# A decoder trunk on one core: the residual's transposes, the next stage's first splits and the last store put in a fixed order

## The chip, the cores and the metric

The kernel runs on one core of one Trainium2 chip. The metric is the device time of one execution in microseconds (us). The core has five instruction queues that run side by side and meet at semaphores: TensorE (PE in the profile), VectorE (DVE), ScalarE (ACT), GpSimd (POOL) and SyncE (SP, which issues most DMA transfers). Each queue runs its own instructions in the order in which the program lists them.

## What is computed

The input is a residual stream of 256 tokens by 2048 columns in float32. Four sub-layers follow one another: a state-space mixer, a SwiGLU feed-forward, differential attention, and a second SwiGLU feed-forward. Each is wrapped the same way: an RMS norm ahead of it, an RMS norm behind it, and an addition to the residual.

```
for sub_layer in (ssd_mixer, swiglu_0, diff_attention, swiglu_1):
    x = x + rmsnorm(sub_layer(rmsnorm(x, w_pre)), w_post)

swiglu(h)         = (silu(h @ w_gate) * (h @ w_up)) @ w_down
diff_attention(u) = heads of (softmax(q1 k1) - lam * softmax(q2 k2)) @ v, normed, @ w_out
```

## The kernel before

**Tiling.** The 256 tokens are two blocks of 128, called t=0 and t=1. A weight matrix arrives as raw tiles of 128 partitions by 4x512 columns. Each is split for the matmul into a rounded part and a remainder: a CAST on ACT writes `hi` (L137), a subtraction on DVE writes `lo` (L138). The numbers behind the names (`hi405`, `lo405`) count these splits. A product over 128 rows of the weights is then three matmuls of 512 columns (L191): rounded activations with `hi`, rounded activations with `lo`, and the activations' remainder with `hi`. The texts call one such matmul a row. A raw tile of four such k-steps gives 12 rows for a token block.

**Helpers.** `mv` (L181) takes a list of weight tiles. For each half tile it issues the rows of t=0 at once and puts those of t=1 on a list, which is let out a few half tiles later (`flush`, with `lag`). After each half tile it calls `tick`, which runs whatever was put off with `later(k, fn)`, k half tiles earlier. `ws` is a second form of matrix product, which the attention uses for its queries and keys. The order of instructions on each queue is worked out when the program is built, from the order of the code, from what each instruction depends on and from a model of durations; `tc.issue_after(ins)` holds an instruction behind another one on the same engine.

**The turn to the next sub-layer.** The last product of a sub-layer (`out_proj`) is gathered in `m`, four pieces n of 512 columns. When the last piece of a token block leaves PSUM, `norm_chain` (L672) runs: DVE makes the mean square `ms_post`, POOL takes its power (`rs_post`, L97), DVE updates the residual `x` in four pieces (L682), PE transposes each piece with four 128x128 transposes into `ptx` (L688), and for each 128 columns ACT writes the rounded half of `xT` (L693) and DVE the remainder (L694). `xT0` to `xT3` are four tiles, and rounded half and remainder of 512 columns lie in the same tile. In the program, the ACT piece j+1 of an `xT` tile waits on a semaphore for the DVE piece j of that same tile. `stats` takes the sum of squares of the new residual, four ACT passes with a scrap output (`junk<-x`, L337), a small DVE reduction (`ssx`, L702), `ms_pre` and POOL's `rs_pre`; the next sub-layer needs it only where its first products leave PSUM. The turn happens three times: mixer to feed-forward, feed-forward to attention, attention to feed-forward. They are called turns A, B and C.

**The attention.** There are four groups of heads. In each, `ws` gives queries and keys (`qk`: an ACT copy L1034, a DVE addition L1035 and, for keys, a DVE multiplication L1038). Scores are small matmuls (L1055) into `sc`. Softmax, transposes of the weights (`pp`) and products with `v` (`po`) follow, put off by fixed numbers of half tiles, while PE works on the next product's rows.

**The end.** The last sub-layer runs the same chain with `final` set: no transposes, and each piece of `x` is stored. Piece n=0 is updated by ACT and POOL (L679, L680), the others by DVE (L682).

## Time and profile before

| | us |
|---|---|
| median of 3 runs | 2509.27 (2509.09 to 2509.4) |
| the profiled execution's own time | 2509.47 |
| its span, first to last instruction | 2507.6 |
| outside the span | 1.87 |
| PE busy | 2489.6 (99%) |
| DVE busy | 1936.8 (77%) |
| ACT busy | 1403.2 (56%) |
| POOL busy | 263.8 (11%) |

In the views of the profile a row of the groups gives line, engine, operation, tiles written and read with the buffer numbers left out, count, busy time, mean duration of one in ns, and the idle time of its engine just before with what ended it. A row of the timeline gives the start in us, the duration, the instruction and its count where neighbours are merged, and in brackets the idle time before it and what released it. Matmuls are pipelined, so the duration of one is longer than the distance from one start to the next, and that distance is what a matmul costs.

### The profile page before, as it was taken

The numbers are of one execution on the slowest core, as the hardware profiler recorded it, in microseconds if no ns is written. First come the engines' busy times: TensorE is split into PE (matmuls) and PEld (weight loads), VectorE is DVE, ScalarE is ACT, GpSimd is POOL, SyncE is SP. The second block draws the span as 40 slices with busy tenths as digits, with TensorE's granted clock in tenths as the row PEclk, the third lists the DMA queues.
The fourth block names the chain that finished last, engine by engine and source line by source line (L and its number), as shares of the span: only waits on it lengthen the run. The fifth ranks groups of instructions, "written<-read, shape, count | busy, mean of one in ns | idle before, by whom it ended". The sixth has DMA issues, their size and how long they took to land.

```text
span 2507.6 us, 31493 instructions
## 1 busy us (share of the span) xinstructions
PE 2489.6 (99%) x11818; PEld 2062.5 (82%) x11818; DVE 1936.8 (77%) x2394; ACT 1403.2 (56%) x1895; POOL 263.8 (11%) x242
## 2 busy tenths in 40 slices
PE   9999999999999999999999999999999999999998
PEld 8888888888888888888888888888888888888886
DVE  6877547777688899978987766556688899879985
ACT  5767546665565455545554654455655465546553
POOL 0131000121110010001001100001100100020002
PEclk9999999999999999999999999999999999999999
DMA  7555555555786786868676544544776967686774
GB/s 287 195 171 199 185 191 195 175 179 192 255 275 202 253 256 215 256 209 265 217 247 237 185 171 144 199 167 143 255 234 207 289 223 232 217 265 225 224 247 151
DMA packets 143385, 541.43 MB, mean 216 GB/s; under 512 B 14400, under 2 KB 31104, under 8 KB 116224
## 3 DMA queue, kind: packets, MB, share of 16 engines
q1 hardware_dynamic: 125872, 503.96, 57.7%
q0 software_dynamic: 16992, 35.13, 7.1%
q8 instruction: 93, 1.52, 0.2%
q14 instruction: 60, 0.49, 0.1%
q10 hardware_dynamic: 368, 0.32, 0.1%
HBM read 520.41 MB, written 18.94 MB: 215 GB/s over the span
## 4 chain that ended last, share of the span: by engine, by line
PE 93%; DVE 2%; issue 1%; ACT 1%; DMA 1%; POOL 0%; SPq 0%; DVEq 0%; ACTq 0%; POOLq 0%
PE acc L265 38%; PE acc L191 33%; PE cp L265 9%; PE acc L239 5%; PE acc L241 2%; PE acc L216 2%; DVE lo L138 1%; PE pt_f L326 1%; ACT hi L137 1%; DMA raw<-in_w_g_dram 1%; PE py L607 1%; PE ptx L688 0%; PE po L1102 0%; PE pc L509 0%; PE px L594 0%
## 5 line engine op out<-in xcount | busy, mean ns | idle before, releaser
L138 DVE TENSOR_TENSOR lo<-raw,hi 128x2048 fp32r<-128x2048 f32 (+2 forms) x401 | 728.8, 1821 | 307.8 <-ACT hi L137 300.9
L137 ACT CAST hi<-raw 128x2048 fp32r<-128x2048 f32 (+2 forms) x401 | 604.6, 1511 | 432.9 <-PE acc L191 122.7
L191 PE MATMUL acc<-hi,xT 128*128 128x512 f32 x1792 | 570.3, 394 | 0.0
L265 PE MATMUL acc<-hi,xT 128*128 128x512 f32 x1608 | 518.7, 390 | 0.1
L191 PEld LDWEIGHTS acc<-hi,xT 128*128 128x128 f32 x1792 | 336.0, 188 | 71.4 <-issue 2.2
L265 PEld LDWEIGHTS acc<-hi,xT 128*128 128x128 f32 x1608 | 301.8, 188 | 63.0 <-DVE sx L748 0.5
L191 PE MATMUL acc<-lo,xT 128*128 128x512 f32 x896 | 351.9, 393 | 1.4 <-DVE lo L138 1.4
L265 PE MATMUL acc<-lo,xT 128*128 128x512 f32 x804 | 313.0, 389 | 0.0
L138 DVE TENSOR_TENSOR lo<-rawm,hi 128x2048 fp32r<-128x2048 f32 (+1 forms) x87 | 181.8, 2089 | 35.0 <-ACT hi L137 33.7
L137 ACT CAST hi<-rawm 128x2048 fp32r<-128x2048 f32 (+1 forms) x87 | 152.7, 1755 | 95.6 <-PE acc L265 54.6
L191 PEld LDWEIGHTS acc<-lo,xT 128*128 128x128 f32 x896 | 168.4, 188 | 37.3 <-DVE lo L138 4.9
L239 PE MATMUL acc<-xT,hi 128*128 128x512 f32 x512 | 181.2, 399 | 0.0
L265 PEld LDWEIGHTS acc<-lo,xT 128*128 128x128 f32 x804 | 150.9, 188 | 31.2
L265 PE MATMUL acc<-hi,ah_f 128*128 128x512 f32 x450 | 176.1, 391 | 0.0
L265 PE MATMUL acc<-hi,al_f 128*128 128x512 f32 x450 | 175.2, 389 | 0.0
L265 PE MATMUL acc<-lo,ah_f 128*128 128x512 f32 x450 | 175.1, 389 | 0.0
L265 PE MATMUL cp<-sh,ff 128*128 128x512 f32 x516 | 172.8, 389 | 0.0
L241 PE MATMUL acc<-xT,lo 128*128 128x256 f32 x512 | 142.9, 280 | 0.0
L142 DVE SCALAR_TENSOR_TENSOR lo<-raw,cols,hi 128x512 fp32r<-128x512 f32 x128 | 93.5, 774 | 56.9 <-ACT hi L141 56.5
L141 ACT ACTIVATE hi<-raw,cols 128x512 fp32r<-128x512 f32 x128 | 84.7, 716 | 64.1 <-PE acc L191 42.2
L239 PEld LDWEIGHTS acc<-xT,hi 128*128 128x128 f32 x512 | 96.1, 188 | 22.7
L265 PEld LDWEIGHTS cp<-sh,ff 128*128 128x128 f32 x516 | 96.9, 188 | 20.1
(305 smaller groups left out, 4081.5 us busy)
## 6 DMA issues: line engine op xcount, KB each, us to landing
raw<-in_w_zxbc_dram SPq DMA_DIRECT2D x77, 1024.0 KB, 4.8
raw<-in_w_d_dram SPq DMA_DIRECT2D x98, 512.0 KB, 5.8
raw<-in_w_g_dram SPq DMA_DIRECT2D x96, 512.0 KB, 6.5
raw<-in_w_u_dram SPq DMA_DIRECT2D x96, 512.0 KB, 5.9
raw<-in_w_qkv_dram SPq DMA_DIRECT2D x48, 1024.0 KB, 4.8
raw<-in_w_so_dram SPq DMA_DIRECT2D x32, 1024.0 KB, 4.8
rawm<-in_w_g_dram SPq DMA_DIRECT2D x64, 512.0 KB, 5.9
rawm<-in_w_u_dram SPq DMA_DIRECT2D x64, 512.0 KB, 6.1
```

The costliest lines, as they stand in the source:

```text
L137: nc.scalar.copy(hi, raw)
L138: nc.vector.tensor_tensor(lo, raw, hi.bitcast(F32), op=ALU.subtract)
L141: nc.scalar.activation(hi[:, j], raw[:, j], AF.Copy, scale=scale[j])
L142: nc.vector.scalar_tensor_tensor(lo[:, j], raw[:, j], scale[j], hi[:, j].bitcast(F32), op0=ALU.mult, op1=ALU.subtract)
L191: nc.tensor.matmul(acc[t], a, b[:, j], start=(i == 0 and j == 0 and q == 0), stop=(i == last and j == 1 and q == 2))
L216: nc.tensor.matmul(acc[job, t], a, b[:, j], start=(i == 0 and j == 0 and q == 0), stop=(i == last and j == 1 and q == 2))
L239: nc.tensor.matmul(acc[ct], hi[:, j, cs], x.rearrange("p a s -> p (a s)"), start=(i == 0 and j == 0), stop=False)
L241: nc.tensor.matmul(acc[ct][:, :S], lo[:, j, cs], x[:, 0], start=False, stop=(i == last and j == 1))
L265: nc.tensor.matmul(acc[k], a, b, start=first and q == 0, stop=last and q == 2)
L326: nc.tensor.transpose(pt[:, j], src[:, j * P:(j + 1) * P], ident)
L607: nc.tensor.matmul(py[e * 64:(e + 1) * 64, a], xd[c][:, 2 * a + e], mts[c][:, 2 * a + e], start=True, stop=True)
```

## The change

Line numbers of the changed kernel differ from those of before: the transposes are L738, the `xT` pieces L744 (ACT) and L746 (DVE), the residual's update L715, the splits L151 and L153, rows L204, scores L1152.

- **Turns, token block 0.** The 16 transposes of t=0 stand behind 12 rows and then six more rows of t=1's last product (eight transposes at each place), through `last_row` and through smaller lags (`lag_last`).
- **Turns, token block 1.** The residual's update is put off by three half tiles, and the transposes stand behind rows of t=0's first product of the next sub-layer. `lag_first` shortens the lags of that product.
- **Pieces of `xT`.** The list `chain` holds each ACT piece behind the piece before it, in the order n=0 j=0..3, n=1 j=0..3 and so on, and each DVE piece likewise. The `lo` of the next product's second tile is held behind the first two tiles' DVE pieces; t=1's last evacuation and its update are held behind the next `lo` splits (`behind`).
- **Statistics.** The four sums of squares are held behind the last ACT piece of their token block; the reduction is held behind the last residual update noted.
- **Attention.** The split of the next product's first tile is held behind the last `qk` copy and multiplication (`held`). Transposes and products of the softmax weights come together, at 9 and 10 half tiles; `lam` is worked out later.
- **End.** The last k-step of t=1 in piece n=3 is done in two halves of 256 columns with accumulators of their own, added to `m` one after the other (`halfway`). All updates are on DVE. The last piece is stored in two halves, and odd pieces are stored from ACT's queue.
- The last activation piece of the feed-forward (`act_piece` in `u_evac`) is put off by three half tiles.

```diff
+def lag_last(i):
+    return 2 if i == 7 else LAG
+def lag_first(i):
+    return (2, 3, 3, 4, 5, 6, 7, LAG)[i]
...
     def norm_chain(t, ss4, last_mw, step, final, t512):
...
+        def update():
+            rn = rstd_of(ss4[:, 3:4], D, f"post{step}_{t}", ss4[:, 0:1])
...
+                    with behind(2 if t and not n and not final else None):
+                            turned[1] = nc.vector.scalar_tensor_tensor(xt[:, cs], mw[:, cs], rn, xt[:, cs], op0=ALU.mult, op1=ALU.add)
+                    if final:
+                        (nc.scalar if n % 2 and not cs.start else nc.sync).dma_start(
...
+        if t and not final:
+            later(3, update)
+        else:
+            update()
+        chain = [None, None]
+        def after(k):
+            return tc.issue_after(chain[k]) if chain[k] else nullcontext()
+        def spread(*ns):
+            for n in ns:
+                with tc.issue_after(last_row[0]):
+                    for j in range(4):
+                        tr = nc.tensor.transpose(...)
+                for j in range(4):
+                    with after(0):
+                        chain[0] = nc.scalar.activation(xT_hi[n][:, j, sl], pj, AF.Copy, scale=sc).ins
+                    with after(1):
+                        chain[1] = nc.vector.scalar_tensor_tensor(xT_lo[n][:, j, sl], ...).ins
+        def spread_first():
+            spread(0, 1)
+            held[seq[0] + 1] = None, chain[1]
+            turned[0] = seq[0]
+            pending.popleft()()
+            spread(2, 3)
         def stats():
+            with after(0):
+                for n in range(4):
+                    row_sumsq(st[:, n:n + 1], xres[(t, n)], t512("junk"))
+            with tc.issue_after(turned[1].ins):
+                nc.vector.tensor_reduce(s1_, st, axis=AX.X, op=ALU.add)
...
-            later(5, stats)
+            if t == 0:
+                later(1, spread_first)
+            else:
+                later(4, lambda: spread(0, 1))
+                later(5, lambda: spread(2, 3))
+            later(6, stats)
...
+            if which:
+                mu = nc.vector.tensor_tensor(dst, dst, rstd_bc, op=ALU.mult)
+                if ct == 3:
+                    held[seq[0]] = cp.ins, mu.ins
...
-        later(6, lambda: turn(0, (0, 1)))
-        later(8, lambda: (turn(1, (0,)), weigh(0)))
-        later(10, lambda: turn(1, (1,)))
-        later(11, lambda: weigh(1))
+        later(9, lambda: (turn(0, (0, 1)), turn(1, (0,)), turn(1, (1,))))
+        later(10, lambda: (weigh(0), weigh(1)))
```

What this does to the queues is shown at three places.

**ACT in turn C, before.** These are the `xT` pieces of t=0 from their first on; `ptx` is the transposed residual, and the number in `xT0` to `xT3` is the tile.

```order
L693 ACTIVATE xT0_99<-ptx_14613,cols_91 128x128
L693 ACTIVATE xT1_100<-ptx_14627,cols_91 128x128
L693 ACTIVATE xT0_99<-ptx_14613,cols_91 128x128
L693 ACTIVATE xT2_101<-ptx_14641,cols_91 128x128
L693 ACTIVATE xT0_99<-ptx_14613,cols_91 128x128
L693 ACTIVATE xT3_102<-ptx_14655,cols_91 128x128
L693 ACTIVATE xT1_100<-ptx_14627,cols_91 128x128
L693 ACTIVATE xT2_101<-ptx_14641,cols_91 128x128
L693 ACTIVATE xT0_99<-ptx_14613,cols_91 128x128
L693 ACTIVATE xT3_102<-ptx_14655,cols_91 128x128
L693 ACTIVATE xT1_100<-ptx_14627,cols_91 128x128
L693 ACTIVATE xT2_101<-ptx_14641,cols_91 128x128
```

**ACT in turn C, now.** The same pieces, with `hi411` a CAST of the next product, `m_14349` the copy of t=1's last accumulator and `junk<-m` its sum of squares.

```order
L744 ACTIVATE xT0_99<-ptx_14634,cols_91 128x128 x4
L744 ACTIVATE xT1_100<-ptx_14647,cols_91 128x128 x4
L744 ACTIVATE xT2_101<-ptx_14666,cols_91 128x128
L867 COPY m_14349<-acc_14560 128x512
L744 ACTIVATE xT2_101<-ptx_14666,cols_91 128x128
L368 ACTIVATE junk_14730,ss_m_14351<-m_14349 128x512
L151 CAST hi411_14809<-raw_14807 128x2048
L744 ACTIVATE xT2_101<-ptx_14666,cols_91 128x128 x2
L744 ACTIVATE xT3_102<-ptx_14679,cols_91 128x128 x4
L368 ACTIVATE junk_14753,ss_x_14752<-x_11149 128x512
```

What moved: before, neighbouring pieces belong to different `xT` tiles; now the four pieces of one tile stand next to each other, x4 in a row, and the first sum of squares of the residual (`junk<-x`) stands behind the last of the 16 pieces.

**DVE in turn C, before.** The rows run from the last piece of t=0 but one to t=1's residual update; `ms_post2_1` is t=1's mean square, `x_11153` and `x_11155` are t=1's residual.

```order
L694 SCALAR_TENSOR_TENSOR xT2_101<-ptx_14641,cols_91,xT2_101 128x128
L138 TENSOR_TENSOR lo409_14708<-raw_14705,hi409_14707 128x2048
L694 SCALAR_TENSOR_TENSOR xT3_102<-ptx_14655,cols_91,xT3_102 128x128
L138 TENSOR_TENSOR lo410_14818<-raw_14815,hi410_14817 128x2048
L719 TENSOR_TENSOR mw_14738<-m_14349,wpost_14490 128x512
L138 TENSOR_TENSOR lo411_14849<-raw_14846,hi411_14848 128x2048
L94 TENSOR_SCALAR ms_post2_1_14740<-ss_m_14351 128x1
L682 SCALAR_TENSOR_TENSOR x_11153<-m_14349,rs_post2_1_14742,x_11153 128x512 x2
L682 SCALAR_TENSOR_TENSOR x_11155<-m_14349,rs_post2_1_14742,x_11155 128x512
```

**DVE in turn C, now.** The same stretch, from the first piece of t=0's third tile to t=1's mean square, behind which its residual update now follows.

```order
L746 SCALAR_TENSOR_TENSOR xT2_101<-ptx_14666,cols_91,xT2_101 128x128
L153 TENSOR_TENSOR lo409_14714<-raw_14711,hi409_14713 128x2048
L746 SCALAR_TENSOR_TENSOR xT2_101<-ptx_14666,cols_91,xT2_101 128x128
L786 TENSOR_TENSOR mw_14732<-m_14349,wpost_14490 128x512
L153 TENSOR_TENSOR lo410_14743<-raw_14740,hi410_14742 128x2048
L746 SCALAR_TENSOR_TENSOR xT2_101<-ptx_14666,cols_91,xT2_101 128x128
L153 TENSOR_TENSOR lo411_14810<-raw_14807,hi411_14809 128x2048
L746 SCALAR_TENSOR_TENSOR xT2_101<-ptx_14666,cols_91,xT2_101 128x128
L746 SCALAR_TENSOR_TENSOR xT3_102<-ptx_14679,cols_91,xT3_102 128x128 x4
L764 TENSOR_REDUCE ssx_14761<-ss_x_14752 128x1
L102 TENSOR_SCALAR ms_pre2_0_14763<-ssx_14761 128x1
L102 TENSOR_SCALAR ms_post2_1_14767<-ss_m_14351 128x1
```

What moved: the three `lo` splits now stand between t=0's pieces of `xT2`, and the reduction `ssx` of t=0's sums of squares, which used to follow t=1's update, stands ahead of t=1's `ms_post` and so of its update.

**PE at the first attention group, before.** `hi355` and `lo355` are the last rows of the keys' product, `hi356` and `lo356` the next product's first tile, `sc0` and `sc1` the scores.

```order
L239 MATMUL acc_11917<-xT3_102,hi355_12034 128x512
L241 MATMUL acc_11917<-xT3_102,lo355_12035 128x256
L191 MATMUL acc_12090<-hi356_12086,xT0_99 128x512
L191 MATMUL acc_12090<-lo356_12087,xT0_99 128x512
L191 MATMUL acc_12090<-hi356_12086,xT0_99 128x512 x2
L191 MATMUL acc_12090<-lo356_12087,xT0_99 128x512
L191 MATMUL acc_12090<-hi356_12086,xT0_99 128x512 x2
L191 MATMUL acc_12090<-lo356_12087,xT0_99 128x512
L191 MATMUL acc_12090<-hi356_12086,xT0_99 128x512 x2
L191 MATMUL acc_12090<-lo356_12087,xT0_99 128x512
L191 MATMUL acc_12090<-hi356_12086,xT0_99 128x512
L1055 MATMUL sc0_12103<-qk_12058,qk_11892 128x256
```

**PE at the first attention group, now.** The names are the same, and `qk_11892`, `qk_12058` and so on are queries and keys.

```order
L270 MATMUL acc_11917<-xT3_102,hi355_12034 128x512
L272 MATMUL acc_11917<-xT3_102,lo355_12035 128x256
L1152 MATMUL sc0_12103<-qk_12058,qk_11892 128x256
L1152 MATMUL sc1_12104<-qk_12058,qk_11892 128x256
L1152 MATMUL sc0_12103<-qk_12058,qk_11892 128x256
L1152 MATMUL sc1_12104<-qk_12058,qk_11892 128x256
L1152 MATMUL sc0_12119<-qk_12073,qk_11905 128x256
L1152 MATMUL sc1_12120<-qk_12073,qk_11905 128x256
L204 MATMUL acc_12090<-hi356_12086,xT0_99 128x512
L1152 MATMUL sc0_12109<-qk_12058,qk_11892 128x128
L1152 MATMUL sc1_12110<-qk_12058,qk_11892 128x128
L1152 MATMUL sc0_12109<-qk_12058,qk_11892 128x128
```

What moved: the first scores come right behind the keys' last row, ahead of the 12 rows of `hi356` and `lo356` that used to stand between them.

More of the change, by code (lines that the diff above doesn't have):

```diff
@@ L136, in prep @@
         if scale is None:
[L137 to L138 removed]
+            ca, cd = held.pop(i, (None, None))
+            with tc.issue_after(ca) if ca else nullcontext():
+                nc.scalar.copy(hi, raw)
+            with tc.issue_after(cd) if cd else nullcontext():
+                los[i] = nc.vector.tensor_tensor(lo, raw, hi.bitcast(F32), op=ALU.subtract)
         else:
@@ L178, in flush, with mv, row @@
             pending.popleft()()
-    def mv(blocks, stat, evac, lag, scale=None, loaded=()):
+    def mv(blocks, stat, evac, lag, scale=None, loaded=(), cut=False):
         acc = {}
         last = 2 * len(blocks) - 1
+        def row(*a, **k):
+            after = last_turn[0]
+            last_turn[0] = None
+            with tc.issue_after(after) if after else nullcontext():
+                return nc.tensor.matmul(*a, **k)
         def run(i, t, hi, lo):
@@ L187, in run @@
                 acc[t] = accp.tile([P, 512], F32, tag="acc", name="acc")
-            for j in range(2):
-                xh, xl = stat(i, j, t)
-                for q, (a, b) in enumerate(((xh, hi), (xh, lo), (xl, hi))):
-                    nc.tensor.matmul(acc[t], a, b[:, j], start=(i == 0 and j == 0 and q == 0),
-                                     stop=(i == last and j == 1 and q == 2))
-            if i == last:
+            end = cut and i == last and t == 1
+            if end:
+                evac(t, acc[t])
+            for cs in (slice(0, 256), slice(256, 512)) if end else (slice(0, 512),):
+                if end:
+                    acc[t] = accp.tile([P, 512], F32, tag="acc", name="acc")
+                for j in range(2):
+                    xh, xl = stat(i, j, t)
+                    for q, (a, b) in enumerate(((xh, hi), (xh, lo), (xl, hi))):
+                        r = row(acc[t][:, cs], a, b[:, j, cs],
+                                         start=((i == 0 or end) and j == 0 and q == 0),
+                                         stop=(i == last - (cut and t == 1 and not end) and j == 1 and q == 2))
+                if end:
+                    evac(t, acc[t], cs)
+            last_row[0] = r.ins
+            if i == last and not end:
                 evac(t, acc[t])
@@ L772, in out_proj, with halfway, evac @@
                     pw(n)
-            def evac(t, ps, n=n):
+            def halfway(t, ps, cs):
+                mt = m[(t, 3)]
+                nc.vector.tensor_tensor(mt[:, cs], mt[:, cs], ps[:, cs], op=ALU.add)
+                if cs.start == 0:
+                    last_mw.append(t512("mw"))
+                    sa = small.tile([P, 1], F32, tag="ss1", name="ssh", bufs=3)
+                else:
+                    sa = ss4[t][:, 3:4]
+                row_sumsq(sa, mt[:, cs], t512("junk")[:, cs])
+                if cs.start == 0:
+                    nc.vector.scalar_tensor_tensor(ss4[t][:, 0:1], sa, 1.0 / D, ss4[t][:, 0:1], op0=ALU.mult, op1=ALU.add)
+                nc.vector.tensor_tensor(last_mw[0][:, cs], mt[:, cs], pw(3)[:, cs], op=ALU.mult)
+                if cs.start:
+                    norm_chain(t, ss4[t], last_mw[0], step, final, t512)
+            last_mw = []
+            def evac(t, ps, cs=None, n=n):
+                if cs is not None:
+                    return halfway(t, ps, cs)
+                if final and n == 3 and t == 1:
+                    nc.vector.tensor_tensor(m[(t, n)], m[(t, n)], ps, op=ALU.add)
+                    return
                 if first:
@@ L779, in evac @@
                 else:
-                    nc.vector.tensor_tensor(m[(t, n)], m[(t, n)], ps, op=ALU.add)
+                    with behind(1 if t and n == 3 and last and not final else None):
+                        nc.vector.tensor_tensor(m[(t, n)], m[(t, n)], ps, op=ALU.add)
                 if not last:
@@ L904, in u_evac @@
             nc.vector.scalar_tensor_tensor(g, ps, rs(t), g, op0=ALU.mult, op1=ALU.mult)
-            acts[(t, 10)] = act_piece(g, f"f{step}_10_{t}")
+            later(3, lambda: acts.update({(t, 10): act_piece(g, f"f{step}_10_{t}")}))
         def kp_stat(kp, j, t):
```

83 lines of the change are left out of this document (40 added, 43 removed).

## The prediction

> **What bounds the kernel now.** The page's first part comes first, then PE's own waits, then the timelines around the places that the change touches. PE is the bound:
>
> ```profile
> PE 2489.6 (99%) x11818; PEld 2062.5 (82%) x11818; DVE 1936.8 (77%) x2394; ACT 1403.2 (56%) x1895; POOL 263.8 (11%) x242
> ```
>
> So time can only go by removing idle PE time or PE work, and the view of PE's waits (who waited for whom: us in total, times, longest) says how much there is:
>
> ```profile
> PE sc L1055 <- DVE qk L1038: 2.8, 4, 0.7
> PE ptx L688 <- DVE x L682: 1.5, 3, 0.7
> PE acc L191 <- DVE lo L138: 1.4, 4, 0.5
> PE ptx L688 <- issue: 0.7, 1, 0.7
> ```
>
> These four sum to 6.4 us: 3.6 at the three turns, if all of the 1.4 for `lo` is put there, and 2.8 in the attention, once per group. In this program a change of order can win those 6.4 us and something behind PE's last matmul, and hardly more. What it can lose has no such bound. The question is therefore whether the new order lets ACT, DVE and POOL keep ahead of PE.
>
> **Turn C, worked out.** First PE's price of a row and of a transpose. In PE's timeline the rows of t=1 run up to the first transposes of t=0:
>
> ```profile
> 1786.20 0.39 PE L191 MATMUL acc<-hi,ah_o 128*128 128x512 f32 x1
> ...
> 1788.47 0.39 PE L191 MATMUL acc<-lo,ah_o 128*128 128x512 f32 x1
> 1789.56 0.63 PE L688 MATMUL ptx<-ident,x 128*128 128x128 f32 x4 [0.70 <-DVE x L682]
> ```
>
> From 1786.20 to 1788.47 lie ten starts, so a row costs 2.27/10 = 0.227 us. For t=1, four transposes and one row between two groups:
>
> ```profile
> 1805.40 0.66 PE L688 MATMUL ptx<-ident,x 128*128 128x128 f32 x4
> ...
> 1806.13 0.60 PE L688 MATMUL ptx<-ident,x 128*128 128x128 f32 x4
> ```
>
> The distance is 0.73, so four transposes cost 0.50. Now what the other engines need. ACT's timeline of the same turn, then its groups between 1786 and 1812:
>
> ```profile
> 1790.22 0.37 ACT L693 ACTIVATE xT<-ptx,cols 128x128 fp32r<-128x128 f32 x1 [0.55 <-PE ptx L688]
> ...
> 1794.34 1.16 ACT L693 ACTIVATE xT<-ptx,cols 128x128 fp32r<-128x128 f32 x4 [0.16 <-DVE xT L694]
> ...
> 1797.93 0.36 ACT L693 ACTIVATE xT<-ptx,cols 128x128 fp32r<-128x128 f32 x1
> ...
> 1801.99 0.63 ACT L337 ACTIVATE junk<-x 128x512 f32<-128x512 f32 x1
> ...
> 1804.35 0.19 ACT L337 ACTIVATION_READ_ACCUMULATOR junk<-x 128x1 f32 x1
> ```
>
> ```profile
> L693 ACT ACTIVATE xT<-ptx,cols 128x128 fp32r<-128x128 f32 x28 | 8.5, 369 | 3.4 <-PE ptx L688 2.9 <-DVE xT L694 0.3
> L137 ACT CAST hi<-raw 128x2048 fp32r<-128x2048 f32 x4 | 7.7, 1913 | 0.8 <-PE acc L191 0.6
> ```
>
> DVE's timeline and its groups between 1797 and 1812, and POOL's timeline:
>
> ```profile
> 1798.32 0.35 DVE L694 SCALAR_TENSOR_TENSOR xT<-ptx,cols,xT 128x128 fp32r<-128x128 f32 x1 [0.24 <-ACT xT L693]
> ...
> 1803.72 0.21 DVE L94 TENSOR_SCALAR ms_post<-ss_m 128x1 f32<-128x1 f32 x1
> 1804.59 2.08 DVE L682 SCALAR_TENSOR_TENSOR x<-m,rs_post,x 128x512 f32<-128x512 f32 x3 [0.67 <-POOL rs_post L97]
> ```
>
> ```profile
> L138 DVE TENSOR_TENSOR lo<-raw,hi 128x2048 fp32r<-128x2048 f32 x3 | 6.9, 2285 | 0.0
> L694 DVE SCALAR_TENSOR_TENSOR xT<-ptx,cols,xT 128x128 fp32r<-128x128 f32 x13 | 3.7, 346 | 0.4 <-ACT xT L693 0.4
> L719 DVE TENSOR_TENSOR mw<-m,wpost 128x512 f32<-128x512 f32 x1 | 0.7, 684 | 0.0
> ...
> L94 DVE TENSOR_SCALAR ms_pre<-ssx 128x1 f32<-128x1 f32 x1 | 0.2, 153 | 0.0
> L702 DVE TENSOR_REDUCE ssx<-ss_x 128x1 f32<-128x4 f32 x1 | 0.1, 149 | 0.0
> ```
>
> ```profile
> 1804.00 0.56 POOL L97 TENSOR_TENSOR rs_post<-ms_post,mhalf 128x1 f32<-128x1 f32 x1 [15.38 <-DVE ms_post L94]
> ```
>
> *One piece.* An ACT piece takes 0.37, a DVE piece 0.35. The piece that ACT starts at 1797.93 ends at 1798.29 and DVE starts its half at 1798.32: a handover of 0.03, and I take the same for the way back. ACT's row at 1794.34 shows that way back: it waited 0.16 for a DVE piece. Before, neighbours belong to different tiles, and these waits almost vanish: four pieces in 1.16 us. In the new order the next ACT piece is always of the same tile, waits for DVE's half, and each step inside a tile costs 0.37 + 0.03 + 0.35 + 0.03 = 0.78. Only at a change of tile can ACT go ahead, at 0.37.
>
> *The 16 pieces of t=0.* Twelve steps of 0.78, three changes of tile at 0.37 and the first piece at 0.37: 9.4 + 1.1 + 0.4 = 10.9. Between them now stand three `lo` splits of 2.29 and the product `mw` of 0.68 on DVE, 7.5 in all. ACT can have one piece done ahead under a split, so two steps of 0.78 overlap: 6.0 are added, and ACT's last piece ends 16.9 after its first began. The CAST of 1.91 that ACT has among these pieces, with a copy and a sum of squares of t=1's, lies under the first two splits.
>
> *What now stands behind the last piece.* The four sums of squares: 1801.99 to 1804.54, so 2.6. Then the reduction (0.15), `ms_pre` (0.15), POOL's `rs_pre` and, behind it, `rs_post` (0.56 each) and about 0.2 of handovers: 1.6. Only then can t=1's `x` be updated, since its `ms_post` stands behind the reduction on DVE. From the update's start to the transposes PE needs 0.8 (1804.59 to 1805.40), from the transposes to ACT's first piece 0.7 (1789.56 to 1790.22). From t=0's first transposes to t=1's: 0.7 + 16.9 + 2.6 + 1.6 + 0.8 = 22.6.
>
> *What PE has to do meanwhile.* In the new order 16 transposes and 48 rows stand between: 4 x 0.50 + 48 x 0.227 = 12.9. PE idles 22.6 - 12.9 = 9.7 us in turn C. It shows partly ahead of rows that read a `lo` (two waits of 1 to 2 us, since `lo409` now stands behind nine pieces and `lo410` behind ten) and mostly, 6 to 7 us in one piece, ahead of t=1's first transposes. Queued behind the waiting transposes on PE are the last 12 rows of the next product's first chunk and everything of t=1.
>
> **Turns A and B.** The program's order is the same there, with two differences: t=1's last evacuation is an addition on DVE, which I price like `mw` at 0.7, instead of an ACT copy; and 51 rows instead of 48 stand in turn A. So A idles 22.6 + 0.7 - 4 x 0.50 - 51 x 0.227 = 9.7, B 22.6 + 0.7 - 12.9 = 10.4. Three turns: 29.8. The 3.6 of waits go. t=1's own 16 pieces come at 0.78 each while PE uses one per three rows, 0.68, and more `lo` splits stand between: between 0 and 2 us in each turn, and I take 0.5, as PE still has rows of t=0's next chunk there. The turns cost 29.8 - 3.6 + 1.5 = **+27.7 us**. Bounds: if ACT gets ahead more under the splits than I allowed, 2 us less per turn; if every split holds it fully, 1.6 more, and with the upper end of t=1's pieces 3 more: +22 to +37 us.
>
> **The attention.** The end of the keys' product in the first group, on PE, ACT and DVE:
>
> ```profile
> 1468.52 0.28 PE L241 MATMUL acc<-xT,lo 128*128 128x256 f32 x1
> ...
> 1471.51 1.80 PE L1055 MATMUL sc<-qk 64*128 64x256 f32 x20
> 1474.01 1.36 PE L1055 MATMUL sc<-qk 64*128 64x128 f32 x12 [0.70 <-DVE qk L1038]
> 1475.30 0.50 PE L191 MATMUL acc<-hi,xT 128*128 128x512 f32 x1
> ```
>
> ```profile
> 1468.14 0.37 ACT L1034 COPY qk<-acc 128x256 f32<-128x256 f32 x1 [0.34 <-PE acc L241]
> 1468.72 1.91 ACT L137 CAST hi<-raw 128x2048 fp32r<-128x2048 f32 x1 [0.21 <-PE acc L239]
> ```
>
> ```profile
> 1468.88 0.75 DVE L1038 TENSOR_TENSOR qk<-qk,rstd_bc 128x256 f32<-128x256 f32 x2
> ```
>
> The wait of 0.70 for the last `qk` multiplication goes. In exchange the next tile's split waits: the last row starts at 1468.52 and ends at 1468.80, ACT copies until 1469.2 (0.37), the CAST of 1.91 ends at 1471.1, the `lo` of 2.29 at 1473.4. Ahead of the first row that reads this `lo` PE has 14 of the 16 scores and one row. The 16 took 1471.51 to 1475.30 less 0.70, 3.1 us; 14 have 2560 of their 3072 columns: 2.6, and with the row 2.8. PE starts them at 1468.64 and is through at 1471.4, two of its three stops (for `qk`, for the CAST) lying inside: it idles 2.0 in all. Per group +2.0 - 0.7 = 1.3. Fewer changes between rows and transposes give back some 0.3 each (an estimate: 0.73 less 0.227 against four times 0.11 is 0.06 a change, at four or five changes). Four groups: **+4 us**, from -2.8 (the wait goes, and nothing comes) to +7 (nothing given back, and 0.5 for the second tile's split).
>
> **The end.** From PE's last matmul to the last store:
>
> ```profile
> 2498.09 0.69 DVE L780 TENSOR_TENSOR m<-m,acc 128x512 f32<-128x512 f32 x1 [1.32 <-PE acc L191]
> ...
> 2500.50 1.42 DVE L682 SCALAR_TENSOR_TENSOR x<-m,rs_post,x 128x512 f32<-128x512 f32 x2 [0.66 <-POOL rs_post L97]
> 2501.30 1.74 POOL L680 TENSOR_TENSOR x<-x,m 128x512 f32<-128x512 f32 x1 [0.83 <-ACT m L679]
> 2501.83 1.75 DVE L682 SCALAR_TENSOR_TENSOR x<-mw,rs_post,x 128x512 f32<-128x512 f32 x1
> ```
>
> Half as many columns to evacuate and square behind the last matmul: an estimate of 0.3 + 0.3 less, from 0.69 for the whole evacuation. Updates: POOL's and DVE's last ran side by side for 1.74 and 1.75 and ended at 2503.58, 3.1 after the start; alone DVE does one in 0.71, so all take 4 x 0.71 = 2.8, 0.3 less. The last store is half as big: 0 to 0.5 less. Against that, 12 matmuls of 256 columns replace six of 512. Their weights' load, from the page's groups:
>
> ```profile
> L191 PEld LDWEIGHTS acc<-hi,xT 128*128 128x128 f32 x1792 | 336.0, 188 | 71.4 <-issue 2.2
> ```
>
> The columns are equal; if the load of 0.188 sets the pace, they cost 12 x 0.188 - 6 x 0.227 = 0.9 more. Together **-0.9 us**, from -1.4 to +0.3. The shifted `act_piece` and `lam` cost nothing: ACT is busy 56% and PE has rows meanwhile.
>
> **The sum.** 27.7 + 4 - 0.9 = +30.8 on the profiled execution's 2509.47 gives 2540.3; the median lies 0.2 under that execution: **2540 us**. With all lower bounds at once it is 2527, with all upper ones 2554.
>
> **The rivals.**
>
> *The chain fits behind PE (faster).* If the pieces alternate without waiting and the sums of squares end early, t=1's update is ready when PE arrives, and all 6.4 us of waits and 0.9 at the end go: 2509.3 - 7.3 = 2502. It decides at a chain of 12.9 us instead of 22.6; t=1's update would have to be ready 10 us earlier. For it: before, 15 of the 16 pieces took 5.3 us (1790.22 to 1795.50). Against it: three splits, `mw`, the sums and the reduction alone are 11.7 on the way.
>
> *Pieces of one tile overlap (slower, but less).* If the wait inside a tile costs ACT nothing, a step is 0.37, and 12 steps save 12 x 0.41 = 4.9 in each turn: 2540 - 14.7 = 2525. Against it stands the wait of 0.16 in ACT's row at 1794.34.
>
> *The idle time slows the clock (slower still).* At the start of the program the 30 warming transposes take 421 ns at the median and 275 at the least, the same instruction:
>
> ```profile
> L363 PE MATMUL pwarm<-ones x30: 275/421/582, 1.3 to 7.0; 128*128 128x128 f32 x30
> ```
>
> They start from 1.3 to 7.0, and by the median more than half of them are slow. If a stop of 6 to 7 us puts PE back to half its pace for some 4 of such 5.7 us, half of that is lost, 2 us for each turn (2.9 at most): 2540 + 6 = 2546. Against it: no stop of that length is in this trace, and rows behind a stop may wait for `xT` anyway. The Trainium skill has a rule for this, in "TensorE: Matmul & The Clock Gate", Part 1 on the HAM clock gate: the array falls to half its clock after an idle window of about 3.4 us and needs about as long a busy one to come back. By that rule this rival holds, at 1.7 us a turn, 2545; the warming transposes agree with its second half, and no run here yet shows the first.
>
> *The chain is barely too long (same).* If it overhangs PE's work by 2 us instead of 9.7 in each turn, and the attention's new stops equal the old, 6 - 3.6 - 0.9 = +1.5 remains: 2511. It needs a chain of 15 us, so pieces that overlap and splits that hide as well.
>
> **How the numbers follow.** A measurement of this kernel can tell about 0.2%, 5 us, from no change. Forecast 0.50, clock 0.20, overlapping pieces 0.13, chain barely too long 0.08, faster 0.09. Slower by over 0.2% is 0.50 + 0.20 + 0.13 = 0.83. The range leaves out the last two cases and the far ends of the others: 2520 to 2552.
>
> **What would show it.** Right: PE's waits list transposes `ptx` behind DVE's `x` at about 6 to 7 us, three times, and rows behind `lo` at 1 to 2 us; ACT's pieces start 0.78 apart with idle time ended by DVE's `xT`; t=1's `ms_post` lies behind t=0's last sum of squares; ahead of the scores no wait over 0.6, ahead of the `lo` row behind them about 1. The clock rival: rows behind the long stop start 0.43 instead of 0.227 apart. Wrong: `ptx` waits under 2 us, or pieces 0.4 apart.

## The result and the profile after

The kernel after takes **2547.7 us** (median of 5 runs, 2546.91 to 2549.35), the kernel before beside it 2509.4 us (5 runs, 2509.09 to 2510.52). The ratio is 1.0152, with a 95% interval of 1.0141 to 1.0164: slower by 38 us. The forecast was 2540 in a range of 2520 to 2552, with 0.83 for slower.

The profiled run took 2546.91 us, 1.8 of them outside its span. The first part of its page, and its mean granted clock:

```profile
PE 2501.5 (98%) x11824; PEld 2069.4 (81%) x11824; DVE 1935.5 (76%) x2402; ACT 1404.7 (55%) x1895; POOL 256.8 (10%) x240
```

```profile
core 0: 2545.1 us, clock 0.994
```

PE is still the bound, but it is busy 12 us longer than before for nearly the same work (six matmuls of 512 columns have become twelve of 256), and the mean clock was 0.999 before. The rest of the 38 us is idle time, which PE's waits name:

```profile
PE ptx L738 <- DVE x L715: 16.7, 3, 6.5
PE acc L204 <- DVE lo L153: 10.7, 7, 2.7
PE acc L204 <- ACT hi L151: 1.8, 4, 0.9
PE acc L247 <- DVE lo L153: 1.7, 2, 1.0
...
PE sc L1152 <- DVE qk L1133: 0.8, 4, 0.2
```

The transposes of t=1 wait three times for the update of `x`, up to 6.5 us. The rows behind a `lo` wait seven times: 2.7 us once in each turn, 0.7 in each of three groups of the attention, and 0.5 once. The lines left out between the last two are a wait of 1.3 at the program's start, which the kernel before has too, and one of 0.8 in turn B, where the attention's `pb` waits for POOL (`PE pb <- POOL dg`); the kernel before has no such wait. The score's wait of 0.7 per group is down to 0.2.

**Where the 38 us lie.** PE's matmuls stand in nearly the same order in both kernels, so the start of the same numbered matmul can be compared. After is later by 0.15 us ahead of turn A (matmul 3320: 679.54 and 679.70), by 10.30 behind it (matmul 4000: 830.52 and 840.82), by 10.34 ahead of B, by 22.15 behind it, in the first group of the attention (matmul 6850: 1457.22 and 1479.37), by 27.61 ahead of C (1770.56 and 1798.17), by 38.21 behind it (1913.03 and 1951.24), and by 38.13 at the last matmul. The steps are A 10.2, B 11.8, attention 5.5, C 10.6, the rest -0.1. From the last matmul's start to the end of the span it is 9.9 before and 9.3 after.

**Turn C in PE's timeline:**

```profile
1817.89 1.03 PE L738 MATMUL ptx<-ident,x 128*128 128x128 f32 x8
...
1828.13 0.50 PE L204 MATMUL acc<-lo,xT 128*128 128x512 f32 x1 [2.63 <-DVE lo L153]
...
1840.90 1.97 PE L738 MATMUL ptx<-ident,x 128*128 128x128 f32 x8 [6.48 <-DVE x L715]
1842.52 0.78 PE L204 MATMUL acc<-hi,xT 128*128 128x512 f32 x1
1843.09 0.63 PE L204 MATMUL acc<-lo,xT 128*128 128x512 f32 x1
1843.52 1.02 PE L204 MATMUL acc<-hi,xT 128*128 128x512 f32 x2
1844.37 0.40 PE L204 MATMUL acc<-lo,xT 128*128 128x512 f32 x1
...
1844.85 1.03 PE L738 MATMUL ptx<-ident,x 128*128 128x128 f32 x8
1845.64 0.48 PE L204 MATMUL acc<-hi,xT 128*128 128x512 f32 x1
```

From t=0's first transposes to t=1's it is 1840.90 - 1817.89 = 23.0 us. Behind the long stop eight transposes take 1842.52 - 1840.90 = 1.62 us, and the next eight, a little later, 0.79. The rows lie 0.43 apart (1843.09 to 1843.52) where it was 0.23. Both stretches together: 0.83 for the transposes and 1.85 - 0.91 = 0.94 for the four rows to 1844.37, 1.77 us lost. The windows of PE say why (length, PE busy, the granted clock, then the share and rate of DMA):

```profile
697.60:704.00 6.40, 5.86 (x14) 0.50 0.63 191
...
711.30:714.40 3.10, 3.10 (x13) 0.50 0.61 252
...
1414.40:1417.40 3.00, 3.00 (x9) 0.50 1.00 344
1424.60:1431.00 6.40, 4.61 (x16) 0.50 0.01 3
1825.60:1828.10 2.50, 0.00 (x0) 1.00 0.00 0
1828.20:1834.00 5.80, 5.63 (x23) 1.00 0.85 271
...
1837.60:1844.00 6.40, 3.10 (x12) 0.50 0.29 120
```

The clock falls to half around a stop of PE and comes back only after some 3.4 us of work or more: in turn A twice (from 697.5 and from 711.2), in B twice (from 1414.3 and from 1424.5), in C once (from 1837.5). The stop of 2.63 us ahead of 1828.13 did not slow it.

**ACT and DVE in the same turn.** ACT's timeline, from t=0's first piece to the last sum of squares, then DVE's:

```profile
1819.90 0.36 ACT L744 ACTIVATE xT<-ptx,cols 128x128 fp32r<-128x128 f32 x1
1820.68 0.37 ACT L744 ACTIVATE xT<-ptx,cols 128x128 fp32r<-128x128 f32 x1 [0.42 <-DVE xT L746]
...
1835.73 0.37 ACT L744 ACTIVATE xT<-ptx,cols 128x128 fp32r<-128x128 f32 x1 [0.42 <-DVE xT L746]
...
1838.35 0.19 ACT L368 ACTIVATION_READ_ACCUMULATOR junk<-x 128x1 f32 x1
```

```profile
1838.57 0.16 DVE L764 TENSOR_REDUCE ssx<-ss_x 128x1 f32<-128x4 f32 x1 [2.09 <-ACT junk L368]
...
1838.84 0.20 DVE L102 TENSOR_SCALAR ms_post<-ss_m 128x1 f32<-128x1 f32 x1
1840.09 2.08 DVE L715 SCALAR_TENSOR_TENSOR x<-m,rs_post,x 128x512 f32<-128x512 f32 x3 [1.05 <-POOL rs_post L105]
...
1851.97 2.29 DVE L153 TENSOR_TENSOR lo<-raw,hi 128x2048 fp32r<-128x2048 f32 x1 [1.74 <-ACT hi L151]
```

Where no `lo` split stands between them, pieces of one tile start 0.78 apart, each waiting 0.42 for DVE's half; at the splits ACT waits longer. The chain of 23.0 us reads off these rows: 2.0 to the first piece, 16.2 for the pieces (1819.90 to 1836.10), 2.5 to the reduction, 1.5 to the update, 0.8 to t=1's transposes.

**A group of the attention**, at the three places where PE waits: the scores that need the last `qk`, the first row of the next product (which reads its `hi`), and the first row that reads its `lo`:

```profile
1491.98 0.70 PE L1152 MATMUL sc<-qk 64*128 64x256 f32 x4 [0.19 <-DVE qk L1133]
1492.99 0.50 PE L204 MATMUL acc<-hi,xT 128*128 128x512 f32 x1 [0.30 <-ACT hi L151]
...
1495.32 0.50 PE L204 MATMUL acc<-lo,xT 128*128 128x512 f32 x1 [0.73 <-DVE lo L153]
```

The wait of 0.70 has become three of 0.19, 0.30 and 0.73. The first three groups come out 0.9 to 1.1 later each.

**The end**, DVE's updates behind the last matmul:

```profile
2538.19 2.08 DVE L715 SCALAR_TENSOR_TENSOR x<-m,rs_post,x 128x512 f32<-128x512 f32 x3 [0.66 <-POOL rs_post L105]
...
2540.18 0.88 DVE L715 SCALAR_TENSOR_TENSOR x<-mw,rs_post,x 128x256 f32<-128x256 f32 x2
```

The four updates take 2.9 us in a row on DVE (2538.19 to 2541.06), 2.8 by the forecast.

### The profile page after: what moved, and what is told of

It reads as the page before. It is cut to its first block, busy times and chain, and to the rows that moved or that the text cites. A ratio compares the mean times of both kernels' runs of the same rounds, so it can differ in the third digit from the quotient of the medians.

```text
span 2545.1 us, 31513 instructions
## 1 busy us (share of the span) xinstructions
PE 2501.5 (98%) x11824; PEld 2069.4 (81%) x11824; DVE 1935.5 (76%) x2402; ACT 1404.7 (55%) x1895; POOL 256.8 (10%) x240
## 4 chain that ended last, share of the span: by engine, by line
PE 93%; DVE 3%; issue 2%; ACT 2%; DMA 1%; POOL 0%; SPq 0%; DVEq 0%; POOLq 0%; ACTq 0%
PE acc L296 38%; PE acc L204 33%; PE cp L296 9%; PE acc L270 5%; PE acc L272 2%; DVE lo L153 2%; PE acc L247 1%; PE pt_f L357 1%; ACT hi L151 1%; PE py L638 1%; DVE xT L746 1%; PE pc L540 0%; PE po L1199 0%; ACT xT L744 0%; ACT junk L368 0%
## 5 line engine op out<-in xcount | busy, mean ns | idle before, releaser
L153 DVE TENSOR_TENSOR lo<-raw,hi 128x2048 fp32r<-128x2048 f32 (+2 forms) x401 | 728.4, 1821 | 258.7 <-ACT hi L151 241.5
L151 ACT CAST hi<-raw 128x2048 fp32r<-128x2048 f32 (+2 forms) x401 | 603.7, 1510 | 405.8 <-PE acc L296 123.7
L204 PE MATMUL acc<-hi,xT 128*128 128x512 f32 x1792 | 573.3, 396 | 1.9 <-ACT hi L151 1.8
L204 PEld LDWEIGHTS acc<-hi,xT 128*128 128x128 f32 x1792 | 339.8, 190 | 76.4 <-ACT hi L151 3.3
L204 PE MATMUL acc<-lo,xT 128*128 128x512 f32 x896 | 354.7, 396 | 10.8 <-DVE lo L153 10.7
L204 PEld LDWEIGHTS acc<-lo,xT 128*128 128x128 f32 x896 | 170.2, 190 | 48.9 <-DVE lo L153 15.8
L153 DVE TENSOR_TENSOR lo<-rawm,hi 128x2048 fp32r<-128x2048 f32 (+1 forms) x87 | 181.8, 2090 | 29.8 <-ACT hi L151 28.6
L151 ACT CAST hi<-rawm 128x2048 fp32r<-128x2048 f32 (+1 forms) x87 | 152.7, 1756 | 93.6 <-PE acc L296 60.9
L329 DVE TENSOR_TENSOR sl<-raw,sh 128x1536 fp32r<-128x1536 f32 x54 | 94.9, 1758 | 25.5 <-ACT sh L326 23.1
```

The source lines that it names most:

```text
L151: nc.scalar.copy(hi, raw)
L153: los[i] = nc.vector.tensor_tensor(lo, raw, hi.bitcast(F32), op=ALU.subtract)
L204: return nc.tensor.matmul(*a, **k)
L329: nc.vector.tensor_tensor(sl[:, 0:3], raw[:, 0:3], sh[:, 0:3].bitcast(F32), op=ALU.subtract)
```

## The experiments

The theory: t=0's chain (pieces at 0.78 with the splits between them, then the sums of squares ahead of t=1's update) sets the time of t=1's transposes, and PE runs out of work. The rivals: the slow clock is a cost of its own; the attention's hold is the bigger part; the places of the transposes (which the expectations call behind 18 and 30 rows) cost by themselves.

**e1: the pieces in free order.** Of the changed kernel:

```diff
-                    with after(0):
+                    if True:
                         chain[0] = nc.scalar.activation(xT_hi[n][:, j, sl], ...).ins
-                    with after(1):
+                    if True:
                         chain[1] = nc.vector.scalar_tensor_tensor(xT_lo[n][:, j, sl], ...).ins
```

> The changed kernel without the fixed order of the 16 xT pieces on ACT and DVE; all else as changed. Chain theory: pieces of different tiles alternate again, 16 of them take about 6 us instead of 10.9, the three lo splits (6.9) and mw (0.7) follow, and ACT's four sums of squares lie under those splits. From t=0's transposes to t=1's: 0.7 + 6.0 + 7.5 + 1.6 + 0.8 = 16.6 us against PE's 12.9, so each turn idles 3.7 instead of 9.7, and no stop is long enough for the slow clock (another 1.7 a turn). 2547.7 - 3 x 7.7 = 2525 us. Rival, the early statistics alone hold t=1's update: the ptx waits stay at 4.6 to 6.8 us and the time at 2545 or more.

Measured: 2523.1 us (2521.09 to 2524.17), ratio 1.0053 [1.0036, 1.0070]. PE's waits:

```profile
PE acc L204 <- DVE lo L153: 8.4, 9, 1.7
PE ptx L738 <- DVE x L715: 5.6, 3, 2.4
```

The fixed order of the pieces alone accounts for 24.6 us of the 38. The stops of the transposes fall from 16.7 to 5.6.

**e2: t=0's statistics behind t=1's update.** The pieces keep their order:

```diff
-            later(6, stats)
+            later(6 if t else 10, stats)
```

> The changed kernel with t=0's sums of squares and their reduction put off by four more half tiles, so that t=1's ms_post and update no longer stand behind them; the pieces stay in the fixed order. Chain theory: four sums (2.6), the reduction, ms_pre and rs_pre (0.9) and the last three steps of 0.78 leave the chain: 22.6 - 5.8 = 16.8 us, an idle time of 3.9 a turn and no slow clock. 2547.7 - 3 x 7.5 = 2525 us, with the waits of 2.6 for a lo still there. Rival, only the order of the pieces matters: under 5 us won, 2543 or more.

Measured: 2534.08 us (2533.35 to 2535.07), ratio 1.0098 [1.0083, 1.0113]. PE's waits:

```profile
PE acc L270 <- ACT v L1114: 2.4, 1, 2.4
PE ptx L738 <- DVE x L715: 1.7, 2, 0.8
```

The stops of the transposes go (16.7 to 1.7), so the sums of squares ahead of the update are the second half of the chain. The forecast was 2525. What it missed: behind turn B the attention's first values need `rs_pre`, and PE waits 2.4 for them and 1.2 in three more waits that follow; its granted clock is 0.50 for 3.4 us behind them (from 1446.5), which costs another 1.7. So turn B takes 10.7 here, A 4.8 and C 4.5.

**e3: both edits.**

> Both together: pieces free and statistics late. Chain theory: 0.7 + 6.0 + the splits up to t=1's update (7.5, with ms_post and rs_post under the last of them) + 0.8 = 15.0 us against 12.9, about 2 us a turn, hardly more than the waits of before. 2509.4 + 3 x 0.9 + 5.5 (attention) - 0.7 (end) = 2517 us. If the places of the transposes behind 18 and 30 rows cost something of their own, it stays above 2525.

Measured: 2518.83 us (2518.48 to 2519.96), ratio 1.0038 [1.0023, 1.0053]; the turns take 2.2, 2.3 and 1.7 and the attention 4.2. With the chain gone, 26.4 of the 28.9 us that it won lie in the turns. That is where most of the 38 us were; the attention's part is e5's.

**e4: PE kept busy in the long stop.** Ahead of t=1's first transposes stand 40 transposes whose result nothing reads:

```diff
+                if t and not n:
+                    fp = aux("fill")
+                    with tc.issue_after(last_row[0]):
+                        for f in range(40):
+                            fl = nc.tensor.transpose(fp[:, :P], ident, ident)
+                    last_row[0] = fl.ins
```

> The changed kernel with 40 more transposes of the identity, whose result nobody reads, ahead of t=1's first ptx transposes in each turn: 40 x 0.11 = 4.4 us of PE work inside a stop of 4.6 to 6.8 us, so the stop itself is no longer than before and PE stands idle for at most 2.4 us in one piece. Clock theory: the slow pace behind the stop (rows 0.43 apart, 8 transposes in 1.62 instead of 0.79) goes, 1.7 a turn, 2547.7 - 5 = 2542.7 us, and the granted clock is 0.999. Rival, rows behind the stop are slow because xT pieces arrive slowly: no difference, 2547.7.

Measured: 2547.35 us (2546.09 to 2550.51), ratio 1.0152 [1.0137, 1.0167]: no gain. Yet the clock was back, 0.998 on the mean, with the long stops' slow rows gone (it fell once more, to 0.50 from 1826.7 to 1830.1, behind the stop of 2.65 in turn C). In turn C, the fill, the transposes behind it and PE's next rows with a wait:

```profile
1833.67 4.53 PE L739 MATMUL fill<-ident 128*128 128x128 f32 x40
1839.56 1.32 PE L744 MATMUL ptx<-ident,x 128*128 128x128 f32 x8 [1.37 <-DVE x L715]
...
1849.24 0.96 PE L204 MATMUL acc<-hi,xT 128*128 128x512 f32 x3 [0.64 <-ACT hi L151]
1851.57 0.50 PE L204 MATMUL acc<-lo,xT 128*128 128x512 f32 x1 [1.13 <-DVE lo L153]
```

PE runs at its full pace behind the stop and then waits 0.64 + 1.13 = 1.77 us for the next splits, as much as the slow clock cost in the kernel after (nothing in the runs makes these two equal). There the split in question ended at 1851.97 + 2.29 = 1854.26 and the row that reads it began at 1854.31: PE came late enough for hardly any wait. By the starts of the same matmuls the turns take 10.9, 9.9 and 11.9 us against 10.2, 11.8 and 10.6, so B gained and A and C lost. The run doesn't say that the clock costs nothing; it says that this edit, which keeps the clock up, wins nothing. The fill also moved some rows on PE and some pieces and splits on ACT and DVE behind t=1's transposes, so what the clock would give back in the unchanged order no run shows.

**e5: the attention as before.** The split of the next product's first tile is no longer held behind `qk`, and the transposes and products of the softmax weights stand at their old places:

```diff
-                    held[seq[0]] = cp.ins, mu.ins
...
-        later(9, lambda: (turn(0, (0, 1)), turn(1, (0,)), turn(1, (1,))))
-        later(10, lambda: (weigh(0), weigh(1)))
+        later(6, lambda: turn(0, (0, 1)))
+        later(8, lambda: (turn(1, (0,)), weigh(0)))
+        later(10, lambda: turn(1, (1,)))
+        later(11, lambda: weigh(1))
```

> The changed kernel with the attention's part undone: the next product's first tile is no longer held behind the qk copies, and transposes and products of the weights come at 6, 8, 10, 11 half tiles as before. Hold theory: PE gained 5.5 us on the kernel of before between the keys' first product and turn C, and all of it goes: 2547.7 - 5.5 = 2542 us, with the waits sc <- DVE qk at 0.7 each back. Rival, it is the later turns and products or lam that cost: those come back too, but then the waits ahead of hi356 and lo356 (0.7 and 1.0 in each group) need not go.

Measured: 2541.64 us (2540.68 to 2543.39), ratio 1.0127 [1.0114, 1.0141]. The attention's part had cost 6.1 us. The old waits are back, and `lam`, which stays late here, costs nothing that shows (the attention takes 0.5 less than before). The run undoes the hold and the later places together, so it doesn't say which of the two cost how much.

PE's wait for `qk`:

```profile
PE sc L1150 <- DVE qk L1133: 2.8, 4, 0.7
```

**e6: the end alone, in the kernel before** (the last chunk in halves, the updates on DVE, two stores on ACT's queue).

> The kernel of before with the change at the end alone: last k-step in two halves of 256 columns, all updates on DVE, last piece stored in two halves, odd pieces from ACT's queue. The distance from PE's last matmul to the end of the span was 9.94 before and 9.31 in the changed kernel: 2509.5 - 0.6 = 2508.9 us. If the 12 half matmuls cost what the weights' load says, it is 2509.8.

Measured: 2509.89 us (11 runs, 2509.17 to 2510.72) beside 2509.73 for the kernel before, ratio 1.0000 [0.9991, 1.0009]. From the last matmul's start to the end it is 9.4 in its trace, 9.9 in that of before. A gain of half a microsecond cannot be told from none.

**e7: the kernel before, with the end's change and a hold on the second tile only.** The split that waits for the last `qk` is the one after the next, which PE needs later. Beside the change's own line:

```diff
-                    held[seq[0]] = cp.ins, mu.ins
+                    held[seq[0] + 1] = cp.ins, mu.ins
```

> The kernel of before with the end's change and with the SECOND tile of the next product, not the first, held behind the last qk copy and multiplication. Hold theory: the CAST that delayed the last qk copy by 1.7 us goes behind it, the 12 rows of the first tile still stand ahead of the scores, and the second tile's lo is ready at 1473.4 against 1474.6 when PE comes to it. So the wait of 0.7 to 0.96 in each of four groups goes and nothing takes its place: 2508.9 - 3.3 = 2505.6 us. If the split of the second tile comes too late, a wait for lo357 of up to 1 us takes its place and the time stays near 2509.

Measured: 2507.29 us (11 runs, 2506.67 to 2507.90), ratio 0.9990 [0.9981, 0.9999]: faster than the kernel before by 2.4 us (forecast 2505.6); all its runs lie below all of that kernel's. PE has all the scores of the first group in one piece:

```profile
1471.63 2.89 PE L1092 MATMUL sc<-qk 64*128 64x256 f32 x32
```

Each group gains 0.5 us on the kernel before. So the hold's idea works, one tile later.

**e8: the changed kernel with all that helped.** Free pieces, late statistics for t=0, no hold on t=0's second split, the second tile's hold, the softmax weights' transposes and products at their old places (as in e5). Left of the change are the places of the transposes, the holds called `behind`, the later `lam` and `act_piece`, and the end.

```diff
-            held[seq[0] + 1] = None, chain[1]
...
-                    with after(0):
+                    if True:
...
-                    with after(1):
+                    if True:
...
-            later(6, stats)
+            later(6 if t else 10, stats)
...
-                    held[seq[0]] = cp.ins, mu.ins
+                    held[seq[0] + 1] = cp.ins, mu.ins
...
```

> The changed kernel with free pieces, late statistics, no hold on the lo of the next product's second tile in the turns, the second tile held in the attention instead of the first and the attention's numbers of before. What is left of the change are the places of the transposes behind 18 and 30 rows and the end. Chain theory: the 3.7 us that both turns and attention still cost in the run with both undone shrink to the waits of before or less: turns 0 to 2 us, attention -3, end -0.6: 2507 us, 2505 to 2509. If the places themselves cost, it stays 2 to 5 us above the kernel with the end and the second tile's hold alone.

Measured: 2512.65 us (11 runs, 2510.50 to 2513.55), ratio 1.0010 [1.0002, 1.0019]. Turns A, B and C cost 3.2, 2.0 and 0.8 us against before, and the attention wins 1.8. PE's largest wait:

```profile
PE ptx L738 <- DVE x L715: 5.4, 2, 2.7
```

What is left of the change costs some 5 us against e7: in turns A and B t=1's transposes still come 2.7 us ahead of their `x`. That it is their places is not shown. In turn B DVE has t=1's mean square only behind the third `lo` split (which waits 1.2 for its CAST and ends at 1410.9) and `mw`, at 1411.7, where e7 has it ahead of that split; so the order ahead of the update may be the cause as well, and no run takes out one without the other.

**e9: only t=1's pieces in free order.**

```diff
-                    with after(0):
+                    with (nullcontext() if t else after(0)):
...
-                    with after(1):
+                    with (nullcontext() if t else after(1)):
```

> The kernel after, with the fixed order of the xT pieces kept for t=0 and taken away for t=1 alone. The prediction gave t=1's own pieces 0.5 us a turn; the three turns came out 4.8 us above it (10.15 + 11.8 + 10.6 against 27.7). Theory: that excess is t=1's pieces, paced at 0.78 and held by the lo splits between them. Then 1.6 us a turn and the stop of 1.2 in the last group's out_proj go: 2547.5 - 4.8 - 1.2 = 2541.5; the three long waits of the transposes stay at 4.6 to 6.8 us, as they come from t=0's pieces. Rival: the excess is t=0's chain or the slow clock behind the long stops, and t=1's pieces are hidden: 2546 to 2548. A third: t=1's pieces in free order are moved by the scheduler with the splits, so that t=0's pieces in the next turn end earlier or later too: then the long waits change by more than 1 us.

Measured: 2544.61 us (2544.48 to 2544.82), ratio 1.0140 [1.0122, 1.0158]: 3.1 us less, neither the theory's 6 nor the rival's 0 to 2. By the starts of the same matmuls the turns gave 1.1 of it and the attention 1.1; in its last group PE's wait of 1.0 for a `lo` ahead of L247 is gone (after: 1.7, 2, 1.0):

```profile
PE acc L247 <- DVE lo L153: 0.7, 1, 0.7
```

The long stops stay (18.5 us in three), and the rows behind them are still slow.

**e10: e4's fill and e9's free order together.** PE's order of e9 is kept but for the 40 transposes in each turn; on ACT and on DVE a dozen instructions stand elsewhere.

> The last two edits together: 40 unused transposes ahead of t=1's first transposes (they keep PE from standing still) and t=1's pieces in free order. Alone the first took 0.3 us back, the second 2.9. Theory: behind the stop two things end at nearly the same time, PE's rows at the slow clock (about 0.8 at the second group of transposes and 0.2 for each of some four rows, 1.6 in all) and the splits that follow t=1's pieces in fixed order; either covers the other, so only both edits together bring the 1.6 of each turn back: 2544.6 - 4.8 = 2540, 2539 to 2542. Rival: the slow rows cost nothing here, for another reason (the pieces of t=1 or the splits stand in the way in free order as well): 2544 to 2545.

Measured: 2538.35 us (2537.97 to 2539.16), ratio 1.0116 [1.0100, 1.0133]. Alone the edits won 0.3 and 3.1, together 9.3: some 6 us come only when both are made. By the starts of the same matmuls, the turns against the kernel before:

| us | A | B | C | sum |
|---|---|---|---|---|
| kernel after | 10.2 | 11.8 | 10.6 | 32.6 |
| e4, clock kept up | 10.9 | 9.9 | 11.9 | 32.7 |
| e9, t=1's pieces free | 10.5 | 10.9 | 10.1 | 31.5 |
| e10, both | 8.4 | 8.4 | 8.9 | 25.6 |

In A and C neither edit alone wins more than 0.5 and both together win 1.8 each; in B the clock alone wins 1.9 and both 3.5. Each row is of one profiled run, and which of the stops of 2.6 us slows the clock differs between them (A and B in the kernel after, C in e4 and e10, A in e9), so single turns are uncertain by a us or more. PE's windows behind the long stops, now filled:

```profile
1424.60:1431.00 6.40, 6.39 (x36) 1.00 0.00 0
1835.00:1840.00 5.00, 4.99 (x29) 1.00 0.82 306
```

And PE's waits, where the list of e4 had 14.7 us in twelve waits for `lo`:

```profile
PE acc L204 <- DVE lo L153: 12.4, 9, 2.7
PE ptx L744 <- DVE x L715: 4.9, 3, 1.9
```

So with t=1's pieces free the slow clock costs 5.9 us in the three turns (e9 to e10), 2.0 a turn, and with the clock kept up t=1's pieces cost 7.1 (e4 to e10), 2.4 a turn, part of which may be e4's moved rows; in the kernel after the one lies for the most part under the other.

## Why the prediction was right, and where not

| term | predicted | measured |
|---|---|---|
| chain, t=0's first transposes to t=1's, A / B / C | 23.3 / 23.3 / 22.6 | 23.1 / 23.2 / 23.0 |
| PE's idle time, A / B / C | 9.7 / 10.4 / 9.7 | 10.2 / 10.2 / 9.3 |
| three turns, net | +27.7 | +32.6 |
| attention | +4 | +5.5 |
| end | -0.9 | -0.6 |
| sum | +30.8 | +37.5 |

**The chain: right, and shown.** Between the first transposes of the two token blocks lie 23.1 us in A (687.86 to 710.99), 23.2 in B (1403.15 to 1426.39) and 23.0 in C. In turn C the terms fit one by one (the forecast in brackets): 0.78 per step, 16.2 for the pieces (16.9), 2.5 for the sums (2.6), 1.5 for the reduction and POOL's two powers (1.6), 0.8 for the update (0.8). Only the way to the first piece was longer, 2.0 instead of 0.7, since ACT has a CAST ahead of it (1818.09 to 1820.0). e1 and e2 cut the chain at its two halves, and the long stops went with either.

The two rivals with a shorter chain fell with these rows: pieces that overlap would start 0.37 apart, and a chain that fits, or nearly so, leaves no stop of 4 to 6 us. One count in the prediction was wrong: turn A has 48 rows between the transposes, like B and C, not 51, so its idle time should have come out as 10.4.

**The stops: right in sum, not in form.** Forecast were two waits of 1 to 2 us for `lo` and one of 6 to 7 for `x`; there was one of 2.7 and one of 4.4 to 6.5. In turn A, PE's two stops were these:

```profile
698.14 0.79 PE L204 MATMUL acc<-lo,xT 128*128 128x512 f32 x1 [2.67 <-DVE lo L153]
...
710.99 1.86 PE L738 MATMUL ptx<-ident,x 128*128 128x128 f32 x8 [4.43 <-DVE x L715]
```

The idle time in the table is the sum of the two (in B 2.68 and 5.81, in C 2.63, 6.48 and 0.16 for an `xT`), with 3.1 added in A and 1.7 in B for rows between the stops that ran at half clock (698.14 to 704.3 and 1414.3 to 1417.6, half of each): there the slow clock lengthened PE's work and shortened its next stop by as much, since t=1's `x` comes when the chain ends, and so it cost nothing.

**The step that failed: that the rows behind the long stop run at full pace.** The likeliest case gave the clock nothing; its rival gave it 2 us a turn, 2546. The rival came about. The clock was at half behind each long stop, for 3.4 us of work in A, 4.9 in B and 3.4 in C; half of that is 5.8 us, against the rival's 6. With the stops' 29.7, less the 3.6 of waits that went, that makes 31.9 of the 32.6 measured; the wait of 0.8 for `pb` in turn B, which the forecast didn't have, is about the rest. The objection raised against it, that rows behind a stop may wait anyway, was right as well in A and C: in e4, with the clock up, PE waits 1.77 there for the next splits. The term for t=1's pieces was mis-sized: 0.5 a turn, in a bound of 0 to 2. Once the clock is restored, their free order wins 7.1 us in the turns (e4 to e10), so they cost up to 2.4 a turn (e4's fill moved some rows too). And once the pieces are free, the clock's return wins 5.9 there (e9 to e10). In the kernel after the two lie over each other, so that the time is near the rival's and not at the sum of all: that it came within 2 us of the rival's 2546 is in part luck. With both taken out, e10's turns sum to 25.6, where the forecast without t=1's 1.5 was 26.2. So the chain was forecast to about a us, and the miss in the turns is what clock and t=1's pieces cost together, 32.6 - 25.6 = 7.0, where the forecast gave 1.5.

The Trainium skill has, in "TensorE: Matmul & The Clock Gate", Part 1, that the clock is judged over windows of 3413 ns that run freely. The trace agrees. These are the half-microsecond stretches in which the clock fell in the kernel after (the number behind the count in brackets is the mean granted clock):

```profile
697.00:697.50 0.50, 0.00 (x0) 0.99 0.00 0
...
711.00:711.50 0.50, 0.50 (x3) 0.65 0.00 0
1414.00:1414.50 0.50, 0.50 (x3) 0.79 0.51 66
1424.50:1425.00 0.50, 0.00 (x0) 0.53 0.00 0
1837.50:1838.00 0.50, 0.00 (x0) 0.54 0.56 229
```

A mean of 0.65 means that the clock was at half for 0.7 of the 0.5 us, so from 711.15. In the same way the others begin at 697.49, 1414.29, 1424.53 and 1837.54. The distances, 13.66, 703.14, 10.24 and 413.01, are 4, 206, 3 and 121 times 3.413. The Trainium skill's table in the same Part also asks for a whole idle window, and there the trace differs: the fall at 697.49 came after 2.0 us of idle time (the row at 698.14 had waited 2.67, since 695.47). The stop of 2.63 ahead of 1828.13 is cut by a window's edge at 1827.30 (three windows ahead of 1837.54), and its 1.8 us inside one window brought no fall. So a stop of 2.6 us slowed the clock in A and B and not in C.

**The attention: right in kind.** Idle time per group was 0.19 + 0.30 + 0.73 = 1.2 where the old wait was 0.7, and three groups came out 0.9 to 1.1 later (forecast 1.3 - 0.3). The waits make 1.2 - 0.7 = 0.5 of these; where the other half comes from was not followed. The last group took 2.3: a further wait of 1.0 for a `lo` in the product behind it, which the forecast didn't have. It is gone in e9, and in e4 too, which keeps the order of t=1's pieces, so that order alone does not bring it; what does stays open. e5 undoes the whole and wins 6.1.

**The end** gained 0.6 in the trace, and e6 shows that this can't be measured. The 12 half matmuls start 0.12 us apart in e6's trace, so the load of 0.188, which the forecast had held against them, doesn't set their pace.

## What to carry to other kernels

A fixed order in which two engines alternate on the same tile costs the full round trip each time (here 0.78 us instead of some 0.3); let neighbours be of different tiles. Put nothing that only a later stage needs ahead of the update that the bounding engine waits for, but look when that stage does need it: put off too far, the statistics stopped PE behind turn B (e2). Where a hold is meant to let an engine finish, hold the work that is needed last: one tile later, with the softmax weights' transposes and products at their old places, the hold came with a gain of 1.8 us where the change's attention had cost 5.5. And when the bounding engine stops, look for two costs of like size behind the stop; removing one of them can show next to nothing (0.3 us) though both together are worth 9.

## What the runs showed of the hardware that was not expected

A stop of PE of which 2.0 us lay inside one window of 3.41 us was enough to halve its clock for the next two windows (697.49 to 704.3). With the long stops the clock fell 3.1 to 4.6 us after PE stood still, and PE ran its first 3.4 to 4.9 us behind the stop at half pace. Forty unused transposes (4.53 us) in each long stop held the clock there. The mean granted clock hardly shows it: 0.994 against 0.999.
